# Dense expert weights of a PEER layer, stored block-major in SBUF and split two blocks at a time

## The chip, the cores and the metric

The kernel runs on one NeuronCore of a Trainium2 chip, as one launch. The metric is the device time of that launch in microseconds (us), the median over runs. The engines are named as the profile names them: PE is TensorE (PEld its weight loads), ACT is ScalarE, DVE is VectorE, POOL is GpSimd, SP is the engine whose queue issues the plain loads. L898 is line 898 of the kernel before; behind the changed place the lines of the changed kernel are up to 10 higher.

## The reference, cut to what matters

One encoder layer: a projection, two attention branches, their merge, and then a PEER layer, a retrieval over 16384 experts of one neuron each. There are 256 tokens (two tiles of 128) and 2048 channels. The part around the change is the PEER layer:

```python
def block(xb):                                   # 8 heads, K = 16 picks per head and token
    qb = (xb @ w_q).reshape(TB, 8, 2, 128)
    s = einsum('thpc,hpnc->thpn', qb, sub_keys)
    sv, si = top_k(s, K)                         # per half of the key
    cand = sv[:, :, 0, :, None] + sv[:, :, 1, None, :]
    cidx = si[:, :, 0, :, None] * 128 + si[:, :, 1, None, :]
    cv, ci = top_k(cand, K);  eidx = cidx at ci  # expert = 128 * i + j
    g = softmax(cv)
    a = gelu(einsum('thkd,td->thk', u_tab[eidx], xb))
    return einsum('thk,thkd->td', g * a, v_tab[eidx])
```

The output is a final RMSNorm of the residual stream with this sum added to it.

## The kernel before, in words

Up to about 1,300 us the kernel does the projections and attention; the change leaves that alone. Then come five stages.

**Tile 0's dots.** For each of a token's 128 picks an indirect DMA, issued by POOL (L751), brings 128 rows of `u_tab` into a ring of six buffers (`g`, `gr`), and DVE multiplies each with `xb` and sums (L754).

**Tile 1's dots, and W0 beside them.** `W0` is a dense 128 x 128 x 128 array in SBUF: for each of the 16384 experts the weight that each token of tile 0 gives it. It is built from one-hots (`build_w0`): per group of four tokens `t4` ACT makes the one-hots (L815, L816, L819), PE multiplies them into a PSUM tile `ps` of 4 tokens x 128 values (L820), and ACT copies that tile to SBUF, `wt[:, t4 * 4:t4 * 4 + 4, :]` (L821). There are 32 such copies, here called evictions. POOL and DVE meanwhile go on with tile 1's gathers and dots. So W0's axes are partition j, token t, block i: the 128 tokens of one block i lie 512 bytes apart.

**W1.** The same for tile 1 (`build_w1`), with the one-hots shared among ACT, POOL and DVE (L831 to L842) and the 32 evictions on ACT again (L845). While it runs, the first `NB0` = 3 blocks of the dense stage are done for tile 0 alone.

**The dense stage** (`dense_v`), for each block i of 128 experts: SP loads 1472 channels of the block's 128 rows of `v_tab` (`vr_`, three buffers, L893). The block's weights of each tile are split into a high part (`wh`, ACT, L898) and the rest (`wl`, DVE, L899), each an instruction of 128 elements that reads `Ws[tt][:, :, i]`, that is, words 512 bytes apart. `vr_` is split in two halves of 736 channels likewise: ACT makes `vhi` (L905); DVE makes `vlo` of the first half (L910), and of the second half DVE makes 420 columns and POOL 316 (L908). PE then does 24 matmuls of 368 columns, for 2 tiles x 4 column groups x 3 products (L915 to L917), into eight PSUM banks that stay open over all blocks.

The last 576 channels are not done densely: `gather_v` brings each of the 2 x 128 picks' rows by an indirect DMA from POOL into four buffers `gv` (L884), and DVE adds them with their weight to `hs` (L887); 256 in all, about two with each block.

**The end.** The first `NB0` blocks are done again for tile 1 (loads and splits included), then comes the final norm, whose scratch rows (`w0_rows`, `gF`) lie in W0's space.

Each engine runs its instructions in program order. That order is made by the framework's scheduler, which simulates the program; splits are written with high priority, so it puts them early. The quoted part that a sentence can't say is how the buffers of the split rotate:

```python
wv = (vp if i % 3 == 2 else bt).tile([P, 2, 2, P], F32R, tag=("b0", "b2", "wv")[i % 3], name="wv")
wh, wl = wv[:, 0], wv[:, 1]
```

Of the kernel before, what the change touches and what calls it, by code (L numbers as in the profile page):

```python
# [10 lines left out]
F32 = mybir.dt.float32  # L11
F32R = mybir.dt.float32r
# [3 lines left out]
AF = mybir.ActivationFunctionType  # L16
# [4 lines left out]
P = 128  # L21
# [19 lines left out]
def block_kernel(ctx: ExitStack, tc: tile.TileContext, A: dict, out: bass.AP):  # L41
    nc = tc.nc

    def pool(name, bufs=1, space=None, side=None, c=ctx):
        kw = {}
        if space is not None:
            kw["space"] = space
        if side is not None:
            kw["side"] = side
        return c.enter_context(tc.tile_pool(name=name, bufs=bufs, **kw))  # L50
# [10 lines left out]
    bt = pool("bt")  # L61
# [9 lines left out]
    def pa(shape):  # L71
        return paux.tile(list(shape), F32, tag="pa", name="pa")
# [76 lines left out]
    for k in range(KT):  # L149
        ps = pa([P, N])  # L150
        for i, (xt, n) in enumerate(xs):
            nc.tensor.matmul(ps[:, i * P:i * P + n], lhsT=xt[:, k * P:(k + 1) * P], rhs=sc[i], start=True, stop=True)
        g = vec[:, gm + k:gm + k + 1]
# [495 lines left out]
    for j in range(8):  # L649
# [10 lines left out]
        for b in range(2):  # L660
            k = 2 * j + b
            g = vec[:, gf + k:gf + k + 1]
# [146 lines left out]
    def build_w0(wt, sT, t4):  # L809
        ps = pa([P, 4, P])  # L810
        oh = wp.tile([P, 2, 4, P], F32, tag="hi", name="oh0", bufs=3)
        for q in range(4):
            t = t4 * 4 + q
            for a in range(2):
                nc.scalar.activation(oh[:, a, q], iota, AF.Abs, bias=sT[:, a, t:t + 1], scale=-1.0)  # L815
        nc.scalar.activation(oh, oh, AF.Relu, bias=onec, scale=-1.0)  # L816
        for q in range(4):
            t = t4 * 4 + q
            nc.scalar.activation(oh[:, 0, q], oh[:, 0, q], AF.Copy, scale=sT[:, 2, t:t + 1])  # L819
            nc.tensor.matmul(ps[:, q, :], lhsT=oh[:, 1, q], rhs=oh[:, 0, q], start=True, stop=True)  # L820
        nc.scalar.activation(wt[:, t4 * 4:t4 * 4 + 4, :], ps, AF.Copy)  # L821

    def build_w1(vp, wt, sT, nj, t4):
        ps = pa([P, 4, P])
        for q2 in range(2):
            oj = bt.tile([P, 2, P], F32, tag="ow", name="oj1", bufs=4)
            t = t4 * 4 + q2 * 2
            m = W1E[(t4 * 2 + q2) % len(W1E)]
            if m == "a":
                for q in range(2):  # L830
                    nc.scalar.activation(oj[:, q], iota, AF.Abs, bias=nj[:, t + q:t + q + 1])  # L831
                nc.scalar.activation(oj, oj, AF.Relu, bias=onec, scale=-1.0)
            elif m == "p":
                for q in range(2):
                    nc.gpsimd.tensor_scalar(oj[:, q], iota, sT[:, 1, t + q:t + q + 1], None, op0=ALU.is_equal)
            else:
                nc.vector.tensor_tensor(  # L837
                    oj, iota.unsqueeze(1).to_broadcast([P, 2, P]), sT[:, 1, t:t + 2].unsqueeze(2).to_broadcast([P, 2, P]),
                    op=ALU.is_equal)
            for q in range(2):  # L840
                oi = vp.tile([P, P], F32, tag="oi1", name="oi1", bufs=4)
                nc.vector.tensor_scalar(oi, iota, sT[:, 0, t + q:t + q + 1], sT[:, 2, t + q:t + q + 1], op0=ALU.is_equal,  # L842
                                        op1=ALU.mult)
                nc.tensor.matmul(ps[:, q2 * 2 + q, :], lhsT=oj[:, q], rhs=oi, start=True, stop=True)
        nc.scalar.activation(wt[:, t4 * 4:t4 * 4 + 4, :], ps, AF.Copy)  # L845

    for h in range(8):
        gather_dots(0, h, eis[0, h])
# [4 lines left out]
    for h in range(8):  # L853
        gather_dots(1, h, eis[1, h])
        for t4 in range(4 * h, 4 * h + 4):
            build_w0(W0, sT0, t4)
# [5 lines left out]
    W1 = w1p.tile([P, P, P], F32, name="W1")  # L862
    vp = pool("vp", side="right")
# [8 lines left out]
    Ws = [W0, None]  # L872
# [3 lines left out]
    def gather_v(n):  # L876
        for _ in range(n):
            if not slots:
                return
            tt, s = slots.pop(0)  # L880
            g = vp.tile([P, DG], F32, tag="gv", name="gv", bufs=NGV)
            if len(slots) >= 2 * P - NGV:
                nc.gpsimd.tensor_copy(g[:, 0:1], W1[:, HW, 0:1])
            nc.gpsimd.indirect_dma_start(out=g, out_offset=None, in_=v_tab,  # L884
                                         in_offset=bass.IndirectOffsetOnAxis(ap=eis[tt, s // 16][:, s % 16:s % 16 + 1], axis=0),
                                         element_offset=DC)
            nc.vector.scalar_tensor_tensor(hs[:, tt, DC:], g, gw[tt][:, s:s + 1], hs[:, tt, DC:], op0=ALU.mult, op1=ALU.add)  # L887

    def dense_v(i, tts, first, last, lo_eng):
        vr_ = vp.tile([P, DC], F32, tag="vraw", name="vr_", bufs=3)  # L890
        if i < 3 and tts == (0,):
            nc.gpsimd.tensor_copy(vr_[:, 0:1], dots[1][:, HD:HD + 1])
        nc.sync.dma_start(vr_, v_tab[i * P:(i + 1) * P, :DC])  # L893
        wv = (vp if i % 3 == 2 else bt).tile([P, 2, 2, P], F32R, tag=("b0", "b2", "wv")[i % 3], name="wv")
        wh, wl = wv[:, 0], wv[:, 1]
        with tc.high_priority():
            for tt in tts:
                nc.scalar.activation(wh[:, tt, :], Ws[tt][:, :, i], AF.Copy)  # L898
                nc.vector.tensor_sub(wl[:, tt, :], Ws[tt][:, :, i], wh[:, tt, :].bitcast(F32))  # L899
        for q in range(2):  # L900
            hi = vp.tile([P, 2 * NB], F32R, tag="vhi", name="vhi", bufs=3)
            lo = vp.tile([P, 2 * NB], F32R, tag="vlo", name="vlo", bufs=3)
            src = vr_[:, q * 2 * NB:(q + 1) * 2 * NB]
            with tc.high_priority():
                nc.scalar.activation(hi, src, AF.Copy)  # L905
                if lo_eng[q] is None:
                    for e_, cs in ((nc.vector, slice(0, LOS)), (nc.gpsimd, slice(LOS, 2 * NB))):
                        e_.tensor_sub(lo[:, cs], src[:, cs], hi[:, cs].bitcast(F32))  # L908
                else:
                    lo_eng[q].tensor_sub(lo, src, hi.bitcast(F32))  # L910
            for tt in tts:
                for n in range(2):
                    o = acc[tt][2 * q + n]
                    ns = slice(n * NB, (n + 1) * NB)
                    nc.tensor.matmul(o, lhsT=wh[:, tt, :], rhs=hi[:, ns], start=first(tt), stop=False)  # L915
                    nc.tensor.matmul(o, lhsT=wh[:, tt, :], rhs=lo[:, ns], start=False, stop=False)  # L916
                    nc.tensor.matmul(o, lhsT=wl[:, tt, :], rhs=hi[:, ns], start=False, stop=last(tt))  # L917


    NB0 = 3  # L920
    HW = 96
    HD = 100
    TE = 6
# [1 line left out]
    NGV = 4  # L925
    for i in range(NB0):
        for t4 in range(32 * i // NB0, 32 * (i + 1) // NB0):
            build_w1(vp, W1, sT1, nj1, t4)
        dense_v(i, (0,), lambda tt: i == 0, lambda tt: False, (nc.vector, None))
    Ws[1] = W1  # L930
    rest = len(slots)
    acc[1] = [paux.tile([P, NB], F32, tag="pa", name=f"acc1_{n}") for n in range(4)]
    for i in range(NB0, P):
        dense_v(i, (0, 1), lambda tt: tt == 1 and i == NB0, lambda tt: tt == 0 and i == P - 1, (nc.vector, None))
        gather_v(max(0, math.ceil(rest * min(1.0, (i - NB0 + 1) / (P - NB0 - TE))) - (rest - len(slots))))
    for i in range(NB0):
        dense_v(i, (1,), lambda tt: False, lambda tt: i == NB0 - 1, (nc.vector, nc.vector))
# [105 lines left out]
```

## Time and profile before

| | |
|---|---|
| median of 3 runs | 2640.59 us (2639.02 to 2647.67) |
| the profiled execution, its own time | 2638.1 us |
| its span, first to last instruction | 2636.3 us |
| tile 0's weights ready, W0 starts on ACT | at 1657 us |
| tile 1's dots end | at 1974 us |
| W1's last eviction | at 2037 us |
| dense stage with both tiles | 2037 to about 2604 us |
| busy over the whole span: PE, DVE, ACT, POOL | 72%, 83%, 44%, 48% |

How to read it: the shares are averages over stages with different limits; DVE's 83%, for one, is 98% in the dense stage and next to nothing for 22 us inside W0's. Busy time also holds time in which an instruction has started and is held up. Instructions of one engine overlap a little at their ends, so what one costs is read from start to start. The clock that the profile lists for PE is the granted one as a share of its full speed.

### The profile page before, as it was taken

How to read it: one execution, taken by the hardware profiler on the slowest of the kernel's cores; microseconds unless marked ns; L12 is line 12 of the kernel's file. 1: busy time of each engine (PE TensorE's matmuls, PEld its weight loads, DVE VectorE, ACT ScalarE, POOL GpSimd, SP SyncE). 2: the span in 40 equal slices, each digit the busy share in tenths (PEclk: the TensorE clock that was granted, in tenths of full speed). 3: DMA queues.
4: the chain of work that ended last, by engine and by line, in shares of the span. 5: the costliest groups of instructions: out<-in, count | busy, mean ns of one | idle time of the engine just before them, and what ended most of it. 6: DMA issues, size and time to landing. Idle time of an engine off the chain costs nothing. (4 is left out here: it accounts for less than half of the span.)

```text
span 2636.3 us, 37183 instructions
## 1 busy us (share of the span) xinstructions
PE 1898.6 (72%) x13809; PEld 1836.1 (70%) x13809; DVE 2180.0 (83%) x3051; ACT 1153.3 (44%) x2206; POOL 1277.3 (48%) x990
## 2 busy tenths in 40 slices
PE   8999999999999999997400000232008999999997
PEld 7999999999999999996400000232007888888896
DVE  4878877557777875569999999996969999999998
ACT  4555544345655544442100000896007454454555
POOL 1333310001111001048876988885837676777785
PEclk9999999999999999998755555565558999999999
DMA  4444445554445465656698999997973888888886
GB/s 163 143 159 168 149 165 187 182 183 160 164 163 171 162 239 179 229 183 236 255 339 331 346 389 422 421 421 289 421 284 120 290 292 286 290 292 291 295 296 247
DMA packets 111059, 659.15 MB, mean 250 GB/s; under 512 B 14531, under 2 KB 17149, under 8 KB 53261
## 3 DMA queue, kind: packets, MB, share of 16 engines
q0 software_dynamic: 59216, 348.40, 34.4%
q1 hardware_dynamic: 51456, 308.21, 33.7%
q8 instruction: 108, 1.77, 0.3%
q14 instruction: 75, 0.61, 0.1%
q10 hardware_dynamic: 204, 0.17, 0.0%
HBM read 653.53 MB, written 2.10 MB: 249 GB/s over the span
## 5 line engine op out<-in xcount | busy, mean ns | idle before, releaser
L186 DVE TENSOR_TENSOR lo<-raw,hi 128x1024 fp32r<-128x1024 f32 x354 | 454.3, 1284 | 244.0 <-ACT hi L185 242.1
L202 PE MATMUL pm<-hT,lo 128*128 128x256 f32 (+1 forms) x2048 | 577.2, 285 | 7.9 <-DVE lo L186 7.9
L200 PE MATMUL pm<-hT,hi 128*128 128x256 f32 (+1 forms) x2048 | 581.1, 285 | 0.0
L201 PE MATMUL pm<-hT,hi 128*128 128x256 f32 (+1 forms) x2048 | 581.0, 284 | 0.0
L185 ACT ACTIVATE hi<-raw 128x1024 fp32r<-128x1024 f32 x374 | 395.9, 1059 | 365.6 <-PE pm L201 294.2
L202 PEld LDWEIGHTS pm<-hT,lo 128*128 128x128 f32 x2048 | 384.2, 189 | 10.7 <-DVE lo L186 9.0
L884 POOL DMA_INDIRECT gv<-in_peer_v_dram,ent x256 | 320.7, 1253 | 142.7 <-DVE hs L887 95.1
L200 PEld LDWEIGHTS pm<-hT,hi 128*128 128x128 f32 x2048 | 385.4, 188 | 0.3
L201 PEld LDWEIGHTS pm<-hT,hi 128*128 128x128 f32 x2048 | 385.4, 188 | 0.2
L916 PE MATMUL acc<-vlo,wv 128*128 128x368 f32 x1024 | 341.3, 346 | 44.6 <-DVE vlo L908 29.0
L754 DVE SCALAR_TENSOR_TENSOR g<-g,xb 128x2048 f32<-128x2048 f32 x128 | 326.3, 2553 | 15.4 <-DMA g<-in_peer_u_dram,ent 15.4
L768 PE MATMUL pa<-cc,gwt 128*128 128x128 f32 x2 | 0.9, 474 | 463.9 <-DVE gwt L764 463.9
L917 PE MATMUL acc<-vhi,wv 128*128 128x368 f32 x1024 | 326.9, 333 | 0.0
L768 PEld LDWEIGHTS pa<-cc,gwt 128*128 128x128 f32 x2 | 0.4, 182 | 464.5 <-DVE gwt L764 464.5
L754 DVE SCALAR_TENSOR_TENSOR gr<-gr,xb 128x2048 f32<-128x2048 f32 x128 | 295.1, 2309 | 29.4 <-DMA gr<-in_peer_u_dram,ent 29.2
L887 DVE SCALAR_TENSOR_TENSOR hs<-gv,gwt,hs 128x576 f32<-128x576 f32 x256 | 303.6, 1186 | 15.3 <-DMA gv<-in_peer_v_dram,ent 14.4
L751 POOL DMA_INDIRECT gr<-in_peer_u_dram,ent x128 | 254.5, 1988 | 81.8 <-DVE gr L754 37.0
L751 POOL DMA_INDIRECT g<-in_peer_u_dram,ent x128 | 250.3, 1956 | 83.1 <-DVE g L754 31.8
L916 PEld LDWEIGHTS acc<-vlo,wv 128*128 128x128 f32 x1024 | 192.1, 189 | 81.4 <-DVE vlo L908 54.8
L898 ACT ACTIVATE wv<-W 128x128 fp32r<-128x128 f32 x256 | 109.4, 429 | 299.4 <-PE acc L917 104.9
L915 PE MATMUL acc<-vhi,wv 128*128 128x368 f32 x1024 | 219.2, 334 | 1.3 <-ACT wv L898 1.1
L917 PEld LDWEIGHTS acc<-vhi,wv 128*128 128x128 f32 x1024 | 192.3, 189 | 0.0
(873 smaller groups left out, 4281.2 us busy)
## 6 DMA issues: line engine op xcount, KB each, us to landing
raw<-in_c_w_in_dram SPq DMA_DIRECT2D x128, 1024.0 KB
raw<-in_c_w_branch_gla_dram SPq DMA_DIRECT2D x16, 1024.0 KB
raw<-in_c_w_branch_diff_dram SPq DMA_DIRECT2D x16, 1024.0 KB
raw<-in_c_w_out_dram SPq DMA_DIRECT2D x16, 1024.0 KB
raw<-in_c_peer_w_q_dram SPq DMA_DIRECT2D x11, 1024.0 KB
gv<-in_peer_v_dram,ent POOLq DMA_INDIRECT x256
raws<-in_c_peer_w_q_dram SPq DMA_DIRECT2D x12, 256.0 KB
xt<-in_x_dram SPq DMA_DIRECT2D x2, 1024.0 KB
```

What stands on the lines that cost most here:

```text
L185: nc.scalar.activation(hi[:, ks], raw, AF.Copy)
L186: (lo_eng or nc.vector).tensor_sub(lo[:, ks], raw, hi[:, ks].bitcast(F32))
L200: nc.tensor.matmul(ps[b], lhsT=wh, rhs=ah, start=(k == 0), stop=False)
L201: nc.tensor.matmul(ps[b], lhsT=wh, rhs=al, start=False, stop=False)
L202: nc.tensor.matmul(ps[b], lhsT=wl, rhs=ah, start=False, stop=(k == KT - 1))
L751: nc.gpsimd.indirect_dma_start(out=g, out_offset=None, in_=u_tab, in_offset=bass.IndirectOffsetOnAxis(ap=ei[:, k:k + 1], axis=0))
L754: nc.vector.scalar_tensor_tensor(g, g, 1.0, xb[:, tt, :], op0=ALU.mult, op1=ALU.mult, accum_out=dots[tt][:, s:s + 1])
L884: nc.gpsimd.indirect_dma_start(out=g, out_offset=None, in_=v_tab, in_offset=bass.IndirectOffsetOnAxis(ap=eis[tt, s // 16][:, s % 16:s % 16 ...
L887: nc.vector.scalar_tensor_tensor(hs[:, tt, DC:], g, gw[tt][:, s:s + 1], hs[:, tt, DC:], op0=ALU.mult, op1=ALU.add)
L915: nc.tensor.matmul(o, lhsT=wh[:, tt, :], rhs=hi[:, ns], start=first(tt), stop=False)
L916: nc.tensor.matmul(o, lhsT=wh[:, tt, :], rhs=lo[:, ns], start=False, stop=False)
L917: nc.tensor.matmul(o, lhsT=wl[:, tt, :], rhs=hi[:, ns], start=False, stop=last(tt))
```

## The change

W0 and W1 keep their size, but their last two axes are swapped: partition j, block i, token t. The evictions (L821, L845) now read the PSUM tile with the token innermost and write 4 neighbouring words per block, one block 512 bytes behind the other. The split reads two blocks at once: `split_w` makes, per pair of blocks and tile, one ACT and one DVE instruction of 256 elements, whose source is contiguous, and `dense_v` calls it at even blocks. The high and low parts lie in buffers of their own, two pairs deep. `NB0` is 2 instead of 3, so it is a whole pair. The element that makes the first `gv` buffers wait (L883) is the same one under its new index.

```diff
 def build_w0 / build_w1
-        nc.scalar.activation(wt[:, t4 * 4:t4 * 4 + 4, :], ps, AF.Copy)
+        nc.scalar.activation(wt[:, :, t4 * 4:t4 * 4 + 4], ps.rearrange("p t i -> p i t"), AF.Copy)
...
+    def split_w(g, tts):
+        def half(pool_, tag):
+            return pool_.tile([P, 2, 2, P], F32R, tag=tag, name="w" + tag)
+        wh, wl = (half(vp, "wv"), half(bt, "b3")) if g % 2 else (half(bt, "b0"), half(bt, "b2"))
+        with tc.high_priority():
+            for tt in tts:
+                src = Ws[tt][:, 2 * g:2 * g + 2, :]
+                nc.scalar.activation(wh[:, :, tt, :], src, AF.Copy)
+                nc.vector.tensor_sub(wl[:, :, tt, :], src, wh[:, :, tt, :].bitcast(F32))
+        return wh, wl
...
 def dense_v
-        wv = (vp if i % 3 == 2 else bt).tile([P, 2, 2, P], F32R, tag=("b0", "b2", "wv")[i % 3], name="wv")
-        wh, wl = wv[:, 0], wv[:, 1]
-        with tc.high_priority():
-            for tt in tts:
-                nc.scalar.activation(wh[:, tt, :], Ws[tt][:, :, i], AF.Copy)
-                nc.vector.tensor_sub(wl[:, tt, :], Ws[tt][:, :, i], wh[:, tt, :].bitcast(F32))
+        if i % 2 == 0:
+            wpair[0] = split_w(i // 2, tts)
+        wh, wl = (w[:, i % 2] for w in wpair[0])
...
-    NB0 = 3
+    wpair = [None]
+    NB0 = 2
```

What this does to the order is seen at two places. The first is DVE in the steady part of the dense stage. Before, two blocks stand there so (`W_15801` is W0, `W_16855` is W1, `vr__20800` and `vr__20846` are the two blocks' rows):

```order
L910 TENSOR_TENSOR vlo<-vr__20800,vhi 128x736
L899 TENSOR_TENSOR wv<-W_16855,wv 128x128
L887 SCALAR_TENSOR_TENSOR hs<-gv,gwt,hs 128x576
L908 TENSOR_TENSOR vlo<-vr__20800,vhi 128x420
L887 SCALAR_TENSOR_TENSOR hs<-gv,gwt,hs 128x576
L899 TENSOR_TENSOR wv<-W_15801,wv 128x128
L910 TENSOR_TENSOR vlo<-vr__20846,vhi 128x736
L899 TENSOR_TENSOR wv<-W_16855,wv 128x128
L887 SCALAR_TENSOR_TENSOR hs<-gv,gwt,hs 128x576
L908 TENSOR_TENSOR vlo<-vr__20846,vhi 128x420
L887 SCALAR_TENSOR_TENSOR hs<-gv,gwt,hs 128x576
L899 TENSOR_TENSOR wv<-W_15801,wv 128x128
```

And two blocks of the changed kernel at the same place of DVE's queue (`wwv` and `wb_20944` are the pair's high and low parts):

```order
L898 TENSOR_TENSOR wb_20944<-W_15801,wwv 128x2x128
L887 SCALAR_TENSOR_TENSOR hs<-gv,gwt,hs 128x576
L898 TENSOR_TENSOR wb_20944<-W_16855,wwv 128x2x128
L919 TENSOR_TENSOR vlo<-vr__20897,vhi 128x736
L917 TENSOR_TENSOR vlo<-vr__20897,vhi 128x420
L887 SCALAR_TENSOR_TENSOR hs<-gv,gwt,hs 128x576 x2
L919 TENSOR_TENSOR vlo<-vr__20941,vhi 128x736
L887 SCALAR_TENSOR_TENSOR hs<-gv,gwt,hs 128x576
L917 TENSOR_TENSOR vlo<-vr__20941,vhi 128x420
```

Four splits of 128 elements per two blocks became two of 256 that stand together, one block ahead of the rows they are used with; the other six kinds of work are the same in number, and POOL's queue keeps its two gathers and one `vlo` per block.

The second place is DVE's queue in the stage of tile 1's dots, at the first weight split (a minus is before, a plus the change):

```order
 L754 SCALAR_TENSOR_TENSOR g,gwt<-g,xb 128x2048 x2
 L754 SCALAR_TENSOR_TENSOR gr,gwt<-gr,xb 128x2048
-L899 TENSOR_TENSOR wv<-W_15801,wv 128x128 x2
...
+L898 TENSOR_TENSOR wb_17189<-W_15801,wb_17188 128x2x128
```

And on ACT, which that split waits for, the end of W0 in the changed kernel:

```order
L819 ACTIVATE oh_16818<-oh_16818,slotT_15811 128x128 x4
L821 ACTIVATE W_15801<-pa 128x128x4 x2
L897 ACTIVATE wb_17188<-W_15801 128x2x128
L897 ACTIVATE wwv<-W_15801 128x2x128
L763 ACTIVATE gwt<-gwt 128x128
```

The split stands in the same place among the dots as before, and behind the last of W0's evictions as before; only its shape is another. On SP's queue the load of `gF` (L942, 1 MB), which stood among the last blocks' loads, now stands between those of blocks 47 and 48, since its space is blocks 32 to 47 of W0.

## Rows read from the trace of the kernel before

**Rows 1.** Busy time by stretch: length, then PE, PEld, DVE, ACT, POOL, PEclk, DMA share, GB/s.

```profile
1657.00:1798.00 141.00, 48.89 (x216) 44.02 (x216) 129.76 (x113) 140.91 (x397) 121.94 (x57) 0.61 1.01 421
1798.00:1820.20 22.20, 9.86 (x42) 9.08 (x42) 0.16 (x2) 20.72 (x55) 1.91 (x2) 0.61 0.44 185
...
1997.00:2025.00 28.00, 25.43 (x172) 22.85 (x170) 28.00 (x100) 26.41 (x65) 17.96 (x31) 1.00 0.02 6
...
2060.00:2590.00 530.00, 493.55 (x2760) 460.10 (x2758) 520.02 (x689) 266.18 (x461) 394.33 (x346) 1.00 0.85 292
```

**Rows 2.** DVE's waits from 1657 us on: total us, times, longest us.

```profile
DVE wv L899 <- ACT wv L898: 23.6, 4, 22.1
DVE hs L887 <- DMA gv<-in_peer_v_dram,ent: 14.4, 25, 1.2
```

**Rows 3.** Timeline of DVE around 1798 us: start, us, engine, line, [idle before, releaser].

```profile
1798.08 0.08 DVE L754 DVE_READ_ACCUMULATOR gr<-gr,xb 128x1 f32 x1
1820.24 0.71 DVE L899 TENSOR_TENSOR wv<-W,wv 128x128 fp32r<-128x128 f32 x2 [22.08 <-ACT wv L898]
```

**Rows 4.** Timeline of ACT at the end of W0.

```profile
1819.17 0.60 ACT L821 ACTIVATE W<-pa 128x512 f32<-128x512 f32 x1 [1.33 <-PE pa L820]
1819.80 0.76 ACT L898 ACTIVATE wv<-W 128x128 fp32r<-128x128 f32 x2
```

**Rows 5.** DVE in the steady dense stage, filtered by line, same columns as rows 1.

```profile
2060.00:2590.00 530.00, 278.84 (x230) 1.00 0.85 292
...
2060.00:2590.00 530.00, 86.82 (x229) 1.00 0.85 292
```

**Rows 6.** Timeline of DVE over a block and a bit of the dense stage.

```profile
2211.30 0.58 DVE L908 TENSOR_TENSOR vlo<-vr__19313,vhi 128x420 fp32r<-128x420 f32 x1
2211.80 0.80 DVE L887 SCALAR_TENSOR_TENSOR hs<-gv,gwt,hs 128x576 f32<-128x576 f32 x1
2212.53 0.37 DVE L899 TENSOR_TENSOR wv<-W,wv 128x128 fp32r<-128x128 f32 x1
2212.83 0.91 DVE L910 TENSOR_TENSOR vlo<-vr__19359,vhi 128x736 fp32r<-128x736 f32 x1
2213.66 0.37 DVE L899 TENSOR_TENSOR wv<-W,wv 128x128 fp32r<-128x128 f32 x1
2213.95 2.13 DVE L887 SCALAR_TENSOR_TENSOR hs<-gv,gwt,hs 128x576 f32<-128x576 f32 x1
```

**Rows 7.** Timeline of POOL beside it.

```profile
2213.03 1.53 POOL L884 DMA_INDIRECT gv<-in_peer_v_dram,ent  x1 [0.30 <-DVE wv L899]
2214.58 0.88 POOL L908 TENSOR_TENSOR vlo<-vr__19359,vhi 128x316 fp32r<-128x316 f32 x1
```

**Rows 8.** Two matmuls of the dense stage, five steps apart in a run without a wait.

```profile
2200.30 0.33 PE L917 MATMUL acc<-vhi,wv 128*128 128x368 f32 x1
...
2201.14 0.33 PE L916 MATMUL acc<-vlo,wv 128*128 128x368 f32 x1
```

**Rows 9.** Single lines: engine, op, count, shortest/median/longest ns, first and last start.

```profile
L764 DVE TENSOR_TENSOR gwt<-gwt x2: 293/293/293, 1655.7 to 1974.7; 128x128 f32<-128x128 f32 x2
L899 DVE TENSOR_TENSOR wv<-W,wv x256: 353/372/2053, 1820.2 to 2615.5; 128x128 fp32r<-128x128 f32 x128
L763 ACT ACTIVATE gwt<-gwt x2: 309/309/309, 1655.3 to 1974.4; 128x128 f32<-128x128 f32 x2
L898 ACT ACTIVATE wv<-W x256: 405/427/499, 1819.8 to 2614.6; 128x128 fp32r<-128x128 f32 x128
L279 ACT ACTIVATE BT<-doT x16: 407/418/419, 626.8 to 918.3; 128x256 fp32r<-128x256 f32 x16
L821 ACT ACTIVATE W<-pa x32: 573/624/700, 1670.5 to 1819.2; 128x512 f32<-128x512 f32 x32
```

**Rows 10.** Two groups of the profile by line and shape: count, busy us, mean ns, idle.

```profile
L837 DVE TENSOR_TENSOR oj<-cc,slotT 128x256 f32<-128x256 f32 x21 | 8.7, 413 | 0.0
L845 ACT ACTIVATE W<-pa 128x512 f32<-128x512 f32 x21 | 12.4, 591 | 1.4
```

More of the change, by code (lines that the diff above doesn't have):

```diff
@@ L844, in build_w1 @@
                 nc.tensor.matmul(ps[:, q2 * 2 + q, :], lhsT=oj[:, q], rhs=oi, start=True, stop=True)
-        nc.scalar.activation(wt[:, t4 * 4:t4 * 4 + 4, :], ps, AF.Copy)
+        nc.scalar.activation(wt[:, :, t4 * 4:t4 * 4 + 4], ps.rearrange("p t i -> p i t"), AF.Copy)
     for h in range(8):
@@ L882, in gather_v @@
             if len(slots) >= 2 * P - NGV:
-                nc.gpsimd.tensor_copy(g[:, 0:1], W1[:, HW, 0:1])
+                nc.gpsimd.tensor_copy(g[:, 0:1], W1[:, 0, HW:HW + 1])
             nc.gpsimd.indirect_dma_start(out=g, out_offset=None, in_=v_tab,
```

## The prediction

> **What bounds the kernel now.** I read the busy time by stretch first, since the shares of the whole span mix stages [rows 1]. The change touches three stretches. In the dense stage (2060 to 2590 us) DVE is busy 520.02 of 530 us and does 115 first-half `vlo` (689 instructions at six per block, rounded by the ends), so a block takes 530 / 115 = 4.61 us; PE's 24 matmuls of a block, 0.84 us for five steps [rows 8], need 24 x 0.168 = 4.03 us, DMA is at 0.85, ACT at half. DVE sets the pace there. While W1 is built (1997 to 2025 us) DVE is busy 28.00 of 28 us, but ACT 26.41: it has 1.6 us to spare and no more. While W0 is built (1657 to 1798 us) ACT is busy 140.91 of 141 us; the DMA runs at 421 GB/s and feeds tile 1's dots. One would take ACT's work there as hidden behind the dots. The waits say otherwise: DVE waits 22.1 us for ACT once [rows 2], and the timeline shows where: after a dot at 1798 us the next thing in DVE's queue is the first weight split, which needs W0 complete [rows 3]; ACT's last eviction starts at 1819.17 and its half of the split at 1819.80 us [rows 4]. Over those 22.2 us the DMA falls to 185 GB/s [rows 1]. The ring of gathered rows is full, so nothing catches up later: every microsecond that ACT's W0 chain gains or loses is one of the kernel.
>
> How DVE spends a block [rows 6], from start to start: the `vlo` of 420 columns 0.50, a `gv` product 0.73, a weight split 0.30, the `vlo` of 736 columns 0.83, the other split 0.29. With a second product that is 0.50 + 2 x 0.73 + 0.59 + 0.83 = 3.38 us. Some 0.09 of the other 1.23 is idle (10 us in 115 blocks); the rest, 1.14 us, is time held up beside POOL: the product at 2213.95 takes 2.13 instead of 0.80 us and ends 0.62 us behind POOL's own `vlo` piece [rows 6, 7].
>
> **The change part by part.**
>
> *The split in pairs, DVE.* Two instructions of 128 elements per block (0.30 + 0.29) become one of 256. A strided 128 costs 372 ns and a contiguous one 293 [rows 9]; 256 contiguous elements cost 413 ns [rows 10], that is 0.34 from start to start with the same overlap of 0.08. So 0.59 - 0.34 = **0.25 us per block**. The bounds: 86.82 us of splits over 115 blocks are 0.755 each [rows 5], against 0.413, so 0.34 if the time that splits were held up goes too; and 0.10 if holding up grows, since DVE's instructions stand in another order beside POOL's unchanged queue and one hold of rows 6 is 1.33 us long. I take 0.25, because held-up time belongs to POOL's instructions, which stay, and falls on whichever DVE instruction comes next. DVE at 4.36 us a block stays above PE's 4.03. Times 125 blocks: -31.3 us (-12.5 to -42.5).
>
> *The split in pairs, ACT.* Two of 427 ns become one of 418 [rows 9] per block; ACT is idle half of that stage, so nothing. The new pair waits until PE has let go the pair two before it, and behind it on ACT stand the `vhi` of the block before its own. PE is done with that old pair a whole block (4 us) before those `vhi` are needed: nothing, unless PE ran four blocks behind.
>
> *The evictions.* 64 of them keep their 512 words, but read PSUM in single words 512 bytes apart and write runs of four words. No row shows either. Below nothing they can't go, as the words are the same in number. Upwards, the nearest row is the strided split: on ACT 427 against 309 ns for 128 words, 0.92 ns a word [rows 9]; for 512 words 0.47 us. Against taking that value: contiguous words cost 0.85 ns on ACT (418 - 309 over 128) [rows 9] and 1.04 on DVE (0.91 - 0.58 over 316) [rows 6], so a strided SBUF word comes to 1.77 on one and 1.04 + 79 / 128 = 1.66 on the other. Nearly the same on engines of different pace, so what is slow is fetching single words from SBUF. PSUM is another memory, which takes 368 words from PE in 0.168 us, 0.46 ns each [rows 8]; that leaves room to hand ACT a word in its 0.85. I take **0**, nearer to the matmul row because it is of the same memory, and keep 0.47 as the other end. At 0.47: 32 x 0.47 = 15.1 us on W0's chain; in W1 21 x 0.47 - 1.6 = 8.3 beyond what ACT has spare [rows 1, 10], and 0.5 for the last eviction, together +23.9 us. The eleven evictions at W1's edges stand where ACT has gaps or loses a block's `vhi`.
>
> [...]
>
> *One front and one back block fewer, one full block more.* Gone from W1's stage: a split and two `vlo`, 0.30 + 0.83 + 0.50 = 1.63 us of DVE, which is the bound there; from the end: 0.30 + 2 x 0.83 = 1.96. Added: a block of 4.36 without its two products (there are 256 of them whatever the number of blocks), 4.36 - 1.46 = 2.90. Sum -0.7.
>
> *`gF` earlier on SP's queue.* It stands behind block 47's load, and what it waits for (W0's blocks 32 to 47 split) comes before what block 48's load waits for. Its 1 MB takes 2.5 us at 421 GB/s in a stage with the DMA at 0.85: nothing, at most 2.5.
>
> **Sum.** 2638.1 (the profiled execution's own time) - 31.3 - 0.7 = 2606.1 us. The median of the runs stands 2.5 us above that execution, so **2609**.
>
> **The rivals.**
>
> 1. *PSUM words cost ACT what SBUF words do.* For: the strided split is the only strided read of ACT in the trace [rows 9]. Against: the pace of the matmuls' writes [rows 8]. The 22.1 us of DVE's wait grow to 37, W1 becomes ACT's, and 23.9 of the 32 us are given back: 2606.1 + 23.9 + 2.5 = 2632.5.
>
> 2. *Slower: the evictions pay on both sides*, reading single words and writing short runs, 0.94 us more each, at the same two places: 32 x 0.94 = 30.1 in W0, 21 x 0.94 - 1.6 = 18.1 in W1, 0.9 at its end, so +49.1: 2655.2 + 2.5 = 2658. It decides from 0.6 us per eviction on (54 x 0.6 - 1.6 = 31), where the dense gain is eaten up. For: ACT has no room in either stage [rows 1]. Against: runs of four are not single words, and a median of 624 ns would have to become 1.56 us [rows 9].
>
> 3. *The dense stage doesn't follow DVE.* The product waits for its gather, whose four buffers turn round in two blocks; DVE already waits 14.4 us for gathers [rows 2], and POOL's pieces hold DVE for 1.14 us a block. If a shorter block only makes those waits longer, the 31.3 us stay: 2638.1 - 0.7 + 2.5 = 2640. Against: 25 waits in 256 products of at most 1.2 us are the sign of a ring that has time left.
>
> That the pairs aren't formed is ruled out by the order, which shows one split of 2 x 128 per pair and tile.
>
> **How the numbers follow.** Forecast 0.50, rival 1 0.32, rival 2 0.10, rival 3 0.08. A measurement of this kernel tells about 0.3% from no change, 7.9 us: faster is below 2632.7, slower above 2648.5. The forecast's own range is 2597 to 2627 (dense gain of 42.5 to 12.5 us), almost all faster: 0.485. Rival 1 lies at the bound, and its dense term has the same width: 0.155 faster, 0.15 the same, 0.015 slower. Rival 2 is 0.09 slower and 0.01 the same, rival 3 0.01 faster, 0.055 the same, 0.015 slower. Together 0.65, 0.23 and 0.12. For 8 in 10 the range takes in the forecast and most of rival 1 and 3: 2597 to 2645; what lies above is rival 2.
>
> **What would show it.** Right: L821 and L845's successors at about 0.6 us; DVE's one wait for ACT still 22 us; the split at 0.41 us with 128 instructions, not 256; the dense block at about 4.36 us with DVE busy above 97%. Rival 1: evictions at 1.0 to 1.1 us and that wait at 37 us, W1's middle with ACT busy throughout and DVE not. Rival 2: evictions near 1.5. Rival 3: evictions unchanged and the block still at 4.6 us, with more of DVE's time held up in L887 or idle for gathers. The prediction is wrong in its base if DVE is idle above 5% in the dense stage while PE is not the bound either.

## The result, and the profile after

The changed kernel took 2617.7 us (median of four, 2609.9 to 2620.6) beside 2644.1 for the kernel before: a ratio of 0.989, interval 0.986 to 0.993. In a second set it was 2611.7 beside 2643.6, 0.989, interval 0.987 to 0.991. Forecast were 2609 and a range of 2597 to 2645; by the prediction's own bound (below 2632.7) the change is faster. The sum was made against the profiled execution (2638.1 us), and there the change gives 2616.4: 21.7 us less, where 32.0 were forecast.

Three marks that both profiles have split the span: the second start of L764 (end of tile 1's dots), the last start of W1's eviction L845, and the end.

| us | to the dots' end | W1 | from there to the end |
|---|---|---|---|
| before | 1974.7 | 62.4 | 599.2 |
| after | 1975.5 | 58.9 | 580.2 |
| difference | +0.8 | -3.5 | -19.0 |
| forecast | 0 | -1.6 | -30.4 |

Busy time by stretch after the change (columns as in [rows 1]: PE, PEld, DVE, ACT, POOL, PEclk, DMA share, GB/s):

```profile
1657.00:1798.00 141.00, 48.97 (x217) 43.76 (x217) 129.40 (x114) 139.45 (x391) 121.93 (x57) 0.61 1.01 421
...
1997.00:2025.00 28.00, 24.50 (x162) 21.66 (x161) 26.88 (x95) 25.38 (x63) 18.64 (x31) 1.00 0.06 14
...
2060.00:2520.00 460.00, 436.51 (x2494) 417.13 (x2493) 433.76 (x517) 204.86 (x314) 340.88 (x309) 1.00 0.89 305
```

The steady stretch again, with the products (L887) and the splits (L898) alone:

```profile
2060.00:2520.00 460.00, 225.67 (x205) 1.00 0.89 305
...
2060.00:2520.00 460.00, 55.49 (x104) 1.00 0.89 305
```

PE's matmuls count the blocks, at 24 each: 2494 / 24 = 103.9 blocks in 460 us, 4.43 us a block, against 2760 / 24 = 115 in 530 us before, 4.61 [rows 1]. DVE's busy time went from 520.02 / 115 = 4.52 to 433.76 / 103.9 = 4.17 us a block, 0.35 less. But its idle time went from 0.09 to (460 - 433.76) / 103.9 = 0.25. About half of what VectorE no longer spends, it now waits.

What it waits for stands in its waits from 1657 us on; against [rows 2], the gathers' share has grown from 14.4 us in 25 waits to 35.0 in 52, and the wait for W0 is as it was:

```profile
DVE hs L887 <- DMA gv<-in_peer_v_dram,ent: 35.0, 52, 1.8
...
DVE wb L898 <- ACT wb L897: 21.7, 1, 21.7
```

The evictions and the splits, line by line, as in [rows 9]:

```profile
L821 ACT ACTIVATE W<-pa x32: 570/606/656, 1672.7 to 1821.3; 128x512 f32<-128x512 f32 x32
...
L845 ACT ACTIVATE W<-pa x32: 577/597/600, 1980.2 to 2034.4; 128x512 f32<-128x512 f32 x32
...
L898 DVE TENSOR_TENSOR wb<-W,wb x64: 409/414/1773, 1822.4 to 2590.0; 128x256 fp32r<-128x256 f32 x64
```

L845 before, whose last start is also the second mark there:

```profile
L845 ACT ACTIVATE W<-pa x32: 573/597/600, 1981.4 to 2037.1; 128x512 f32<-128x512 f32 x32
```

The evictions cost what they did (L821's median 606 ns after 624, L845's 597 in both), although they read PSUM in words 512 bytes apart. The split of 256 costs the 0.41 us forecast as a median; in the steady stretch, where some are held up, it is 55.49 / 104 = 0.53 on the mean. The wait itself, on DVE's timeline in two consecutive blocks:

```profile
2213.71 0.92 DVE L919 TENSOR_TENSOR vlo<-vr__19342,vhi 128x736 fp32r<-128x736 f32 x1
2215.23 2.19 DVE L887 SCALAR_TENSOR_TENSOR hs<-gv,gwt,hs 128x576 f32<-128x576 f32 x1 [0.60 <-DMA gv<-in_peer_v_dram,ent]
2217.34 0.58 DVE L917 TENSOR_TENSOR vlo<-vr__19342,vhi 128x420 fp32r<-128x420 f32 x1
2217.85 0.80 DVE L887 SCALAR_TENSOR_TENSOR hs<-gv,gwt,hs 128x576 f32<-128x576 f32 x1
2218.58 0.75 DVE L898 TENSOR_TENSOR wb<-W,wb 128x256 fp32r<-128x256 f32 x2
2219.25 0.91 DVE L919 TENSOR_TENSOR vlo<-vr__19389,vhi 128x736 fp32r<-128x736 f32 x1
2220.09 1.42 DVE L917 TENSOR_TENSOR vlo<-vr__19389,vhi 128x420 fp32r<-128x420 f32 x1
2221.43 1.66 DVE L887 SCALAR_TENSOR_TENSOR hs<-gv,gwt,hs 128x576 f32<-128x576 f32 x2
```

And POOL beside it:

```profile
2214.94 0.95 POOL L884 DMA_INDIRECT gv<-in_peer_v_dram,ent  x1 [0.30 <-ACT wb L897]
2215.91 0.88 POOL L917 TENSOR_TENSOR vlo<-vr__19342,vhi 128x316 fp32r<-128x316 f32 x1
```

In the block without splits DVE reaches its first product 0.60 us before the row is there, and the product is then held for 2.19 instead of 0.80 us, until 0.63 us behind POOL's subtraction (its end is at 2216.79). Both kinds of loss, the wait and the hold, are in this one product. Four questions follow: which part of the change gave what, whether the gather ring took the rest, what holds VectorE up, and whether W0's wait is worth what the prediction said.

### The profile page after: what moved, and what is told of

Same layout as the page of the kernel before. It is cut to its first block, busy times and chain, and to the rows that moved or that the text cites. A ratio compares the mean times of both kernels' runs of the same rounds, so it can differ in the third digit from the quotient of the medians.

```text
span 2614.6 us, 37107 instructions
## 1 busy us (share of the span) xinstructions
PE 1889.1 (72%) x13809; PEld 1835.5 (70%) x13809; DVE 2132.0 (82%) x2921; ACT 1106.8 (42%) x2076; POOL 1266.1 (48%) x989
## 5 line engine op out<-in xcount | busy, mean ns | idle before, releaser
L884 POOL DMA_INDIRECT gv<-in_peer_v_dram,ent x256 | 309.6, 1209 | 140.9 <-DVE hs L887 87.1
L926 PE MATMUL acc<-vhi,wb 128*128 128x368 f32 x1024 | 334.2, 331 | 0.8 <-DVE wb L898 0.8
L887 DVE SCALAR_TENSOR_TENSOR hs<-gv,gwt,hs 128x576 f32<-128x576 f32 x256 | 280.3, 1095 | 39.3 <-DMA gv<-in_peer_v_dram,ent 35.0
L926 PEld LDWEIGHTS acc<-vhi,wb 128*128 128x128 f32 x1024 | 192.4, 189 | 1.0 <-DVE wb L898 1.0
L925 PE MATMUL acc<-vlo,wb 128*128 128x368 f32 x512 | 172.9, 342 | 18.0 <-DVE vlo L917 9.2
L925 PE MATMUL acc<-vlo,wwv 128*128 128x368 f32 x512 | 172.3, 341 | 15.0 <-DVE vlo L917 10.4
L820 PE MATMUL pa<-oh 128*128 128x128 f32 x256 | 58.1, 408 | 104.2 <-ACT oh L819 102.8
```

## The experiments

Each was timed four to six times beside the kernel before on its chip. "Under" is the difference of the medians, the ratio stands with its interval. Blocks are counted as above, from 2060 to 2520 us (to 2500 in the two changed kernels whose five buffers end the stage earlier). They come from one profiled execution each, whose own time lies up to 9 us from the median of its runs (the last row's is the farthest, and the slowest of its five); over 126 blocks that is up to 0.07 us a block.

| kernel | under before, us | ratio | block, us | DVE busy + idle, us a block |
|---|---|---|---|---|
| changed, again | 31.9 | 0.989 (0.987 to 0.991) | 4.41 | 4.17 + 0.24 |
| pairs, old layout | 16.2 | 0.994 (0.993 to 0.996) | 4.47 | 4.32 + 0.16 |
| layout alone | 40.3 | 0.984 (0.982 to 0.986) | 4.28 | 4.08 + 0.20 |
| pairs offset by a block | 33.9 | 0.988 (0.986 to 0.990) | 4.36 | 4.08 + 0.28 |
| changed, 5 buffers | 71.4 | 0.973 (0.972 to 0.975) | 4.11 | 3.97 + 0.14 |
| layout alone, 5 buffers | 73.1 | 0.973 (0.971 to 0.974) | 4.05 | 3.98 + 0.07 |
| before, 5 buffers | 24.3 | 0.991 (0.990 to 0.993) | 4.52 | 4.51 + 0.01 |
| changed, no POOL piece | 56.3 | 0.979 (0.977 to 0.980) | 4.23 | 3.54 + 0.69 |
| layout alone, no POOL piece | 38.6 | 0.985 (0.983 to 0.987) | 4.44 | 3.61 + 0.83 |

**The two parts of the change.** The pairs alone, against the changed kernel; the evictions are again those of the kernel before:

```diff
...
-                src = Ws[tt][:, 2 * g:2 * g + 2, :]
+                src = Ws[tt][:, :, 2 * g:2 * g + 2].rearrange("p t i -> p i t")
```

> The split in pairs alone: W stays slot-major, so a split fetches 2 x 128 single words, and the evictions are as in the kernel before. Theory A (the price of a DVE instruction decides, fixed part and strided words): a strided 256 costs 413 + 2 x (372 - 293) = 571 ns, 0.49 us from start to start, so a block saves 0.59 - 0.49 = 0.10 us of the 0.25 and the kernel stands 12 us under the one before; evictions at 0.6 us as before. Theory B (any shorter split is eaten by gathers and held-up time): the block stays at 4.6 us and the time within 4 us of before. Theory C (the split's order, not its length, brought the gain): the time is that of the changed kernel, 22 to 26 us under before.

The layout alone, against the kernel before; the evictions are those of the change, and `NB0` is 3:

```diff
...
-                nc.scalar.activation(wh[:, tt, :], Ws[tt][:, :, i], AF.Copy)
+                nc.scalar.activation(wh[:, tt, :], Ws[tt][:, i, :], AF.Copy)
...
```

> The block-major layout alone: one block per split as before, three front blocks as before, 128 contiguous words. Theory A: a split costs 293 instead of 372 ns, so a block saves 2 x 0.079 = 0.16 us, the dense stage 0.16 x 125 = 20 us, and nothing is saved at the front; 20 us under before. Theory B: 4 us at most. Theory C (the order): within 4 us of before. By all three the evictions read PSUM in words 512 bytes apart and stay at 0.6 us, as they do in the changed kernel.

The pairs alone came 16.2 us under, near theory A's 12; their strided split takes 605 ns, where A had 571:

```profile
L898 DVE TENSOR_TENSOR wb<-W,wb x64: 582/605/1696, 1820.9 to 2594.8; 128x256 fp32r<-128x256 f32 x64
```

The layout alone came 40.3 us under, twice what A gave, and more than the whole change. Its splits cost 278 ns, 94 less than the strided ones:

```profile
L899 DVE TENSOR_TENSOR wv<-W,wv x256: 273/278/2011, 1821.1 to 2576.8; 128x128 fp32r<-128x128 f32 x128
```

```profile
2060.00:2520.00 460.00, 447.11 (x2579) 431.33 (x2577) 438.85 (x644) 224.55 (x432) 359.71 (x320) 1.00 0.91 316
...
2060.00:2520.00 460.00, 234.12 (x214) 1.00 0.91 316
```

The second row is the products alone. DVE's busy time fell by 0.44 us a block, from 4.52 to 4.08. The two splits make 2 x 0.094 = 0.19 of that, which is A's term; the rest is time in which DVE is no longer held up, above all in the products, from 2.42 to 234.12 / 107.5 = 2.18 us a block. A had left that out.

So each part pays alone, 16.2 and 40.3 us, but they don't add up: on top of the new layout, pairing costs some 8 to 14 us. With it come two front blocks instead of three, other buffers and another order on DVE; these weren't taken apart. B and C both fall. The changed kernel itself was timed once more, beside three of the runs below:

> The changed kernel once more, beside the following three on one chip, so that they are compared with it there: 22 to 28 us under before.

It came 31.9 us under, a little more than the first set's 26.4; the intervals of the two ratios overlap.

**The gather ring.** W1's one-hots use the `gv` buffers before the gathers do, so that a fifth fits:

```diff
-                oi = vp.tile([P, P], F32, tag="oi1", name="oi1", bufs=4)
+                oi = vp.tile([P, DG], F32, tag="gv", name="oi1", bufs=NGV)[:, :P]
...
-    NGV = 4
+    NGV = 5
```

> The changed kernel with five buffers for the gathered rows instead of four (the one-hots of W1 take the same buffers before them, to fit). Theory A (the ring of four, which turns in two blocks, is what kept the block at 4.42 instead of 4.36 us): DVE's waits for gathers in the dense stage fall from 30 to under 10 us, the block to 4.2 to 4.3 us (PE is busy 4.20 us a block, no less is possible), and the kernel is 12 to 25 us faster than the changed one, 35 to 50 under before. Theory B (gathers are late because GpSimd issues them late, behind its own part of the correction or held beside VectorE): the waits stay at about 30 us and the time is the changed kernel's, 22 to 26 us under before.

```profile
2060.00:2500.00 440.00, 437.17 (x2571) 432.24 (x2570) 425.50 (x534) 210.22 (x324) 365.57 (x319) 1.00 0.92 328
...
2060.00:2500.00 440.00, 192.81 (x212) 1.00 0.92 328
```

DVE's waits for gathers in the steady stretch, in the changed kernel and with five buffers, and the last eviction of W1 here:

```profile
DVE hs L887 <- DMA gv<-in_peer_v_dram,ent: 21.3, 36, 1.4
...
DVE hs L887 <- DMA gv<-in_peer_v_dram,ent: 5.0, 11, 1.3
...
L845 ACT ACTIVATE W<-pa x32: 577/597/599, 1975.8 to 2023.1; 128x512 f32<-128x512 f32 x32
```

Theory A, by more than it asked: 71.4 us under before, 40 to 45 better than the changed kernel. Gather waits of DVE in the steady stretch fell from 21.3 to 5.0 us and PE is busy 437.17 of 440. But the waits are the smaller part of it: of the 0.32 us that a block lost, 0.11 is idle time and 0.20 busy time, in which DVE is held up less; the products went from 2.17 to 192.81 / 107.1 = 1.80 us a block. The block is 4.11 us, by 0.08 above PE's floor of 4.03; the 4.20 that the expectation named as the floor was too high. Some 7 us of the whole gain are no matter of the gathers: W1's stage is 52.0 instead of 58.9 us long (from 1971.1 to 2023.1), and five buffers for its one-hots are all that the edit gives it. From there to the end, at 2569.7, it is 546.6 us. Is the ring the kernel's trouble from the start, or only since the change?

> The kernel before with five gather buffers and nothing else. Theory F (the ring of four binds only once the change has shortened VectorE's block: before, VectorE is idle 0.08 us a block and waits for nothing else): at most 0.08 x 125 = 10 us faster than before. Theory G (the ring costs the kernel before as well, not as idle time but in products held up beside GpSimd, whose gathers and correction pieces it sets in step with them): held-up time of the products falls from 0.84 to about 0.2 us a block as it does with the change, the block comes to about 4.2 us, and the kernel is 40 to 55 us faster than before; the change is then worth only what is left to PE's floor, 15 to 30 us.

```profile
2060.00:2520.00 460.00, 432.00 (x2441) 407.62 (x2440) 459.18 (x611) 236.55 (x406) 349.08 (x307) 1.00 0.87 299
...
L845 ACT ACTIVATE W<-pa x32: 576/597/599, 1978.3 to 2027.2; 128x512 f32<-128x512 f32 x32
```

24.3 us under, between the two theories. The profiled execution, 18.1 us shorter, tells where: 7.0 in W1 (62.4 to 55.4, the side effect), 8.1 behind it (599.2 to 591.1, with the end at 2618.3), 2.9 ahead. Behind W1 that is theory F: DVE's idle time goes to nothing and its busy time stays at 4.51 us; G's fall of the held-up time did not come. So the ring had little to lose before, and much after: behind W1 the change is worth 19.0 us with four buffers and 591.1 - 546.6 = 44.5 with five.

**Why single splits did better than pairs.** In the changed kernel two splits stand in every second block. Here tile 1's pairs start one block later, so each block has one:

```diff
...
+        for tt in tts:
+            if wcur[tt] is None or i in (0, NB0) or i >= wcur[tt][2] + 2:
+                wcur[tt] = split_w(tt, i - 1 if tt and i == NB0 else i)
...
```

> The changed kernel, but tile 1's pairs begin one block after tile 0's, so that each block has one split of 2 x 128 instead of every second block two of them; same words, same number of instructions, four gather buffers. Theory D (uneven spacing: in a block without splits VectorE reaches the next product before its row has landed, and the ring of four has no spare buffer to cover it): VectorE's idle time falls from 0.27 to 0.19 us a block or less, as in the layout alone, its busy time stays near 4.1, the block comes to 4.2 to 4.3 us and the kernel 40 to 55 us under before. Theory E (it is the long split itself, held up beside GpSimd, that costs more than two short ones): the time of the changed kernel, within 5 us.

33.9 us under, within 2 of the changed kernel, as theory E has it; idle time did not fall (0.28). Theory D falls. That the long split is what costs, as E says, is not shown by it. The second test, single splits with five buffers, 73.1 under, is as good as pairs with five:

> The layout alone (single-block splits, three front blocks) with five gather buffers. Theory D: with a spare buffer the spacing no longer matters, and single splits have only their dearer fixed part against the pairs, at most 0.09 us a block, 11 us, and PE's 4.2 us a block caps both: the time is 0 to 11 us above that of the changed kernel with five buffers, 60 to 71 us under before. Theory E: singles keep the 16 us they had over pairs with four buffers, 85 us under before or PE's floor of 4.1 us a block.

```profile
2060.00:2500.00 440.00, 440.00 (x2606) 439.52 (x2605) 432.02 (x649) 225.73 (x437) 371.84 (x324) 1.00 0.94 333
```

PE is busy in all of the 440 us, so both forms stand at its floor there and the test can't part them. Next, POOL's 316 columns of `vlo` were given to DVE (the expectations call `vlo` the correction; the columns are of the second half, though they say the first):

```diff
-                if lo_eng[q] is None:
+                if lo_eng[q] is None and LOS < 2 * NB:
...
-                    lo_eng[q].tensor_sub(lo, src, hi.bitcast(F32))
+                    (lo_eng[q] or nc.vector).tensor_sub(lo, src, hi.bitcast(F32))
...
-    LOS = 420
+    LOS = 736
```

> The changed kernel with the first-half correction all on VectorE (736 columns there, none on GpSimd); four buffers. VectorE pays 0.91 - 0.58 = 0.33 us more a block. Theory H (VectorE's held-up time, 1.0 us a block, is made by GpSimd's two-input subtraction): the held-up time falls under 0.3 us, the block to about 4.42 + 0.33 - 0.75 = 4.0 to 4.1 us, PE's floor, and the kernel is 35 to 50 us faster than the changed one. Theory I (it is made by the tails of GpSimd's gathers): held-up time stays near 1 us, the block comes to about 4.7 us, 35 to 45 us slower than the changed one.

The steady stretch, and the products in it:

```profile
2060.00:2520.00 460.00, 448.19 (x2612) 438.49 (x2610) 385.15 (x542) 215.85 (x330) 301.04 (x216) 1.00 0.91 320
...
2060.00:2520.00 460.00, 176.32 (x216) 1.00 0.91 320
```

A product takes 176.32 / 216 = 0.82 us, instead of 225.67 / 205 = 1.10: the held-up time is gone, with two gathers a block still on POOL. That is theory H's mechanism. Its size fell short, 24 to 30 us under the changed kernel and not 35 to 50, and the block is 4.23 us, not 4.0 to 4.1: DVE now waits for gathers, 69.9 us of this stretch instead of 21.3. This trace also has the time of a gather from its issue to its landing, 6.8 us as a median:

```profile
DVE hs L887 <- DMA gv<-in_peer_v_dram,ent: 69.9, 80, 3.2
...
gv<-in_peer_v_dram,ent POOLq DMA_INDIRECT x216, 6.8
```

Four buffers turn round in two blocks, 2 x 4.23 = 8.5 us. The 6.8 leave 1.7 of that for the product, 0.82, and for POOL to come to the next issue: by this estimate the ring has next to nothing left. Before the change two blocks were 2 x 4.61 = 9.2 us.

The same edit on the layout alone:

> The layout alone (single-block splits) with the first-half correction all on VectorE; four buffers. With GpSimd's subtraction gone, held-up time is gone in both forms. Theory J (single splits beat pairs by 10 to 16 us because VectorE is held up 0.15 us less a block beside that subtraction): the advantage goes with it, and the time is that of the pairs without GpSimd's piece, 50 to 62 us under before, or up to 9 us above it for the dearer splits. Theory K (single splits stand between the products and give the ring of four a better spacing): the advantage stays, 66 to 75 us under before, with less idle time than the 0.68 us a block of the pairs.

```profile
2060.00:2520.00 460.00, 435.49 (x2488) 423.62 (x2488) 373.87 (x621) 215.48 (x417) 297.78 (x206) 0.99 0.88 305
...
DVE hs L887 <- DMA gv<-in_peer_v_dram,ent: 82.3, 75, 3.5
```

Only 38.6 us under, about what it was with POOL's piece (40.3): DVE is held up no longer (its 206 products there take 167.71 us, 0.81 each), but waits 82.3 us for gathers. Without POOL's piece the pairs are ahead by 56.3 - 38.6 = 17.7 us. K falls. Of theory J the direction came true, but it allowed 9 us at most. So with four buffers single splits led only while DVE was held up beside POOL's subtraction. Why the hold falls on them more lightly, and why the idle time without it is 0.83 against 0.69 us, the runs don't say.

**W0's wait, and the best version.** The first split is held back behind a late dot product:

```diff
+        if g == 0 and tts == (0,):
+            nc.gpsimd.tensor_copy(wl[:, 0, 0, 0:1], dots[1][:, HD:HD + 1])
```

> The changed kernel with VectorE's first weight split held back until a late dot product of tile 1 is done, so that it can't stand in VectorE's queue waiting for W0. Theory A (that wait is on the path in full): the wait of 21.7 us at 1800 to 1822 us is gone, the dots end 21.7 us earlier, and so does the kernel: 43 to 48 us under before. Theory A2 (the dots are fed by the DMA, which moved 185 instead of 421 GB/s in those 22.2 us, so that only the missed transfers come back): 22.2 x (1 - 185 / 421) = 12.4 us faster than the changed kernel, 34 to 39 under before. Theory B (the stall is made up later, since the dots wait for gathers anyway): the changed kernel's time.

47.9 us under (ratio 0.981, 0.980 to 0.983), 16 to 22 better than the changed kernel. Its dots and their end:

```profile
1798.00:1822.00 24.00, 7.84 (x34) 7.36 (x35) 22.14 (x21) 23.89 (x67) 20.95 (x11) 0.59 1.01 422
```

```profile
L764 DVE TENSOR_TENSOR gwt<-gwt x2: 292/292/292, 1660.4 to 1958.7; 128x128 f32<-128x128 f32 x2
```

The wait is gone, the DMA stays at 422 GB/s, and from L764 to L764 it takes 298.3 instead of 317.6 us (1657.9 to 1975.5), 19.3 us less. One pair of traces can't give that to a microsecond, as the second trace of the changed kernel shows, with 313.0 for the same stage:

```profile
L764 DVE TENSOR_TENSOR gwt<-gwt x2: 292/292/293, 1656.0 to 1969.0; 128x128 f32<-128x128 f32 x2
```

The eleven traces here without the held split take 313.0 to 319.0 us, 315.8 on the mean, and the three with it (two more follow) 296.4 to 299.4, 298.0 on the mean. So some 18 of the 21.7 us come back: theory A in the main, and the 12.4 us by missed transfers were too few. All together, with the pairs offset, and then without pairs (layout alone, all three first splits held, five buffers):

> The changed kernel with all three edits that took a wait away: pairs offset by a block, the first splits held behind a late dot product of tile 1, five gather buffers. If the parts add up as far as PE lets them: the 71 us of five buffers under before plus the 19 to 24 us of the held split, the offset adding nothing more since PE already paces the block at 4.2 us: 88 to 97 us under before. Rival: the 21.7 us come back as another wait (W1's stage starts earlier but its gathers or GpSimd's one-hots don't): 70 to 80 under before.

> The layout alone, with five buffers and the first three splits held behind the late dot product: no pairs. If pairs bring nothing once the dense stage runs at PE's pace: the time of the kernel with pairs offset, held and five buffers, within 6 us, some 85 to 95 under before. If pairs still bring something at the front, where VectorE paces W1: 5 to 10 us above it.

88.0 us under (2555.6; ratio 0.967, 0.966 to 0.968) and 96.0 under (2549.2; 0.964, 0.962 to 0.965). The parts add up, and the simpler kernel, with no pairs in it, is the fastest of the study, by 8 us where its expectation had at most 6. It is the layout of the change with two waits taken away; pairing has no part in it.

## Why the prediction was right, and where it was not

The time, its sign and its range came out right. The term of the dense stage was mis-sized: -30.4 us from W1's end on, where -19.0 were measured (-21.0 in the second trace of the changed kernel). What is inside it was wrong twice, in opposite directions, and that the two partly cancel is luck: DVE's busy time fell by 0.35 us a block instead of 0.25, and its idle time grew by 0.17 instead of not at all.

- **The evictions at nothing**: right in the value, and the evictions that read single words of PSUM cost ACT no more than those that read runs (L821's median 606 ns after 624, L845's 597 in both). The argument for it, that the matmuls' writes leave PSUM room, no run tests. Rivals 1 and 2, with 0.42 of the chance, both died on this one row.
- **The price of the split**: right at 0.41 us for 256 words as a median, a little high for 128 (0.29 forecast, 0.28).
- **ACT's pairs at nothing**: right. From 1657 us on DVE waits for ACT's half once, and that is W0's wait (the row of 21.7 us above).
- **"Held-up time belongs to POOL's instructions, which stay, and falls on whichever DVE instruction comes next"**: right in the main. It belongs to POOL's subtraction, as the run without that piece shows, and most of it stays: unhindered, a block would now cost DVE 3.38 - 0.25 = 3.13 us, so 4.17 - 3.13 = 1.04 of the 1.14 us are left. But it moved: the products went from 278.84 / 115 = 2.42 [rows 5] to 225.67 / 103.9 = 2.17 us a block, the splits from 0.755 to 0.53, and DVE's `vlo`, which is what remains of its busy time, from 1.34 to 1.47. With five buffers it falls further (4.17 to 3.97 busy).
- **"25 waits in 256 products of at most 1.2 us are the sign of a ring that has time left"**: this is the step that failed. DVE waited seldom only because it was slow: five buffers were worth 8 us from W1's end on before the change and 34 after it. With 0.35 us less to do, DVE waits 0.25 us a block, 0.17 more, and the block falls by 0.18 (4.61 to 4.43; 4.36 was forecast). Rival 3 had the mechanism, as all or nothing; it took half. The sign that the prediction set for itself, DVE idle above 5% while PE isn't the bound, came true: 26.24 of 460 us, 5.7%. So DVE alone no longer sets the pace, which is what the sum took for granted.
- **PE's floor of 4.03 us**: right, the five-buffer kernels stop at 4.05 to 4.11.
- **The ends**: W1 gave 3.5 us instead of 1.6 (58.9 us in both traces of the changed kernel). It comes with the pairs and the front block that they save, and not with the layout: the stage takes 59.0 us in the pairs on the old layout (1973.4 to 2032.4) and 62.0 in the layout alone (1972.1 to 2034.1), which keeps three front blocks. Why it is twice the forecast, no run tells.
- **"Every microsecond that ACT's W0 chain gains or loses is one of the kernel"**: taking the wait away brings some 18 of 21.7 us, so nearly. A shorter or longer W0 chain was not tried.
- **`gF` earlier on SP's queue**: not measured by itself.

## What to carry to other kernels

Before crediting a shorter instruction on the bounding engine, work out the period of every ring that it consumes from (here 6.8 us from a gather's issue to its landing, and the product, against the 8.5 us of two blocks in which four buffers turn round): a ring that is waited for seldom today may be only a little faster than the engine, and then it is the next bound (DVE's waits for gathers were 14.4 us before the change and 35.0 after, from 1657 us on). Try the buffer count beside the change; from W1's end on, a fifth buffer was worth 580.2 - 546.6 = 34 us here after it and 8 before. Measure the parts of a change alone, and each on top of the other: layout and pairing both paid alone, and together they gave less than the layout.

## What was not expected of the hardware

A product of VectorE that meets GpSimd's subtraction ends 0.62 and 0.63 us behind it in the two rows shown, after 2.13 and 2.19 instead of 0.80 us. Beside GpSimd's gathers alone no product is held: of 216 in the stretch without the subtraction, with 216 gathers beside them, the longest takes 836 ns.

```profile
L887 DVE SCALAR_TENSOR_TENSOR hs<-gv,gwt,hs x216: 805/817/836, 2061.1 to 2518.4; 128x576 f32<-128x576 f32 x108
```

The product at 2213.95 starts 0.63 us ahead of the subtraction's recorded start, while a gather still runs on GpSimd, and still ends behind it [rows 6, 7]. Why, no run shows.

ScalarE's eviction of 512 words takes 0.60 us (L845's median, 597 ns in both kernels) whether it reads PSUM in order, as before, or reads one word in 128 and writes SBUF in runs of four, as after the change. From SBUF, a stride of 128 words costs ScalarE 427 - 298 = 129 ns for 128 words (298 is its split in the layout alone):

```profile
L898 ACT ACTIVATE wv<-W x256: 289/298/314, 1820.7 to 2575.0; 128x128 fp32r<-128x128 f32 x128
```

So ScalarE pays for single words in its splits from SBUF and, by these medians, not in its evictions from PSUM. VectorE pays for them in SBUF too, 372 - 278 = 94 ns for 128 words; no row here has it reading single words of PSUM.
